# A transformer layer with 32 routed experts: gathers issued at other places, the long form of one expert in line, and a weight ring of 19 slots in place of 17

## The chip, the cores and the metric

The kernel runs on one core of one Trainium2 chip. The metric is device time in microseconds of one execution. The kernel before has a median of 1142.95 us over three runs (1142.18 to 1146.23).

## What is computed

One decoder layer over 256 tokens of width 1024 in float32: a mixer (three kinds of attention, a convolution, an output projection), a LayerNorm, and a mixture of 32 experts, of which each token takes four, closed by a second LayerNorm. The experts are what this case is about:

```python
def moe_ffn(x, router_w, router_b, w_gu, b_gu, w_down, b_down):
    t = x.reshape(B * L, D)
    logits = (t @ router_w + router_b).astype(jnp.float32)
    top_val, top_idx = lax.top_k(logits, TOP_K)            # TOP_K = 4
    wts = jax.nn.softmax(top_val, axis=-1)
    gates = jnp.sum(jax.nn.one_hot(top_idx, N_EXPERTS) * wts[..., None], axis=1)
    for e in range(N_EXPERTS):                             # 32
        gu = t @ w_gu[e] + b_gu[e]                         # 1024 x 2048
        gate = jnp.minimum(gu[:, ::2], SWIGLU_LIMIT)
        up = jnp.clip(gu[:, 1::2], -SWIGLU_LIMIT, SWIGLU_LIMIT)
        h = (up + 1.0) * gate * jax.nn.sigmoid(gate * SWIGLU_ALPHA)
        out = out + gates[:, e:e + 1] * (h @ w_down[e] + b_down[e])   # 1024 x 1024
```

The weights of an expert are 12 MB. The router is skewed: with these inputs the largest expert has 161 tokens, two have none, and those two are neither loaded nor computed.

## The kernel before

The mixer comes first; its instructions are scheduled by hand in one stream per engine. `order` (L868) then ranks the experts by their number of tokens on the chip. The experts run in an order of ranks that is fixed in `_ORDER` (L86) and cut into 14 batches; below, e0, e1, ... are places in that order. A batch is one, two or four experts that share one gather, and `HOME` is how many groups of 32 tokens (passes) of each the gather covers: four for an expert that is alone, two in a pair, one in a batch of four. The first batch is e0 alone (92 tokens here, three passes), the second is e1 to e4 (ranks 13, 17, 21 and 25, one pass each), the third is e5 alone: rank 1, 161 tokens, six passes, more than its home of four.

**The weights.** An expert's weights are 12 tiles of 1 MB ("loads" below), c0 to c7 for the first product and c8 to c11 for the second. They go through a ring of 17 slots in SBUF: `RING` = 16 (L41), and `wx` (L820), which is allocated after the mixer; one of the 16 holds the rows `res` of the first LayerNorm until the accumulator is built from it. e0's 12 loads are issued by the mixer's `prefetch`, which keeps `KEEP` = 6 slots free for the mixer itself. From e1 on SP issues every load in order (`load`, L1446; the DMA is L1450), each behind a wait for the slot's last reader (`released`, L977, on PE's counter `REL`).

**An expert.** `place(e)` (L1319) issues what belongs to the place and then `either` (L1010) branches by the expert's number of tokens to one of two forms of `passes` (L1334): the short one for at most `HOME` passes, which stands in line, or the long one, which stands behind the whole program (`put_behind`, L1025) and branches back. In a form PE does the first product for all passes (`up`, L1058), transposes h (`h_trans`, L1094), and does the second product (`down`, L1107); DVE and ACT do the activation between them (`act`, L1075) and evacuate the result to `ys` (`evacuate`, L1133). `bias` (L1049) opens a bank with a one-hot tile `sels[e % 4]`, which POOL writes.

**Gather and scatter.** Tokens are gathered by matmuls with a one-hot matrix: DVE writes P (`start_batch`, L1156), PE multiplies in two halves of 16 matmuls (`gather_next`, L1312, at L859) and DVE evacuates to `XG` (L865). DVE also writes P times the gates, PG (`start_gates`, L1169); PE transposes it (`gates_of`, L1208) and, at the next batch's first expert, scatters `ys` with it (`scatter_before`, L1219), which DVE adds to `acc` (L1226). For an expert with more tokens than its home there is a second set: Px, PGx (`gates_x`, L1274), the gather into `XGx` (`gather_x`, L1262) and `scatter_x` (L1285). `gates_x` is issued at the place of each expert with a home of four, and PE's short form of such an expert begins with a wait for it:

```python
            elif h == 4 and t_:
                take(X, PPX)
                take(X, PGRX)
            for ks in ((0, 1), (2, 3), (4,)):
```

The gather of the next batch is issued in the last expert of a batch, between `act` and `h_trans`; in e5's long form `gather_x` and `scatter_before` come first.

Of the kernel before, what the change touches and what calls it, by code (L numbers as in the profile page):

```python
# [34 lines left out]
L, D, E, SLOTS = 256, 1024, 32, 32  # L35
# [2 lines left out]
LAMBDA_INIT = 0.8 - 0.6 * math.exp(0.0)  # L38
NEG = -1e30
BIG = 3e38  # L40
RING = 16  # L41
SLOT = 2048
KEEP = 6
CT = 16
# [47 lines left out]
NPASS = [-(-min(L, 4 * L // max(1, _r)) // 32) for _r in SIGMA]  # L92
NR = RING + 1
TAIL = 3
B_DOWN = 9
WARM5 = 8


# [65 lines left out]
def body(ctx, tc, nc, A, out):  # L164
# [650 lines left out]
    def one(name, *shape, dt=F32):  # L815
        return mo.tile([128, *shape], dt, name=name)
# [23 lines left out]
    PGx = one("PGx", 2, 2, 4, SLOTS)  # L840
    hs = [one(f"h{i}", 256) for i in range(2)]
    gc = one("gc", 256)
    sels = [one(f"sel{i}", 128) for i in range(4)]

    ysx = [t.rearrange("p (n a) b -> p n (a b)", n=4) for t in XGx]
    pgTx = hT8[:, 4:8].rearrange("p s j t -> p (s j) t")
# [150 lines left out]
    def program(X, kind):  # L997
# [9 lines left out]
        def more(e, p):  # L1007
            return X.If(count(e) > p * SLOTS)

        def either(e, near, far, here):  # L1010

            name, here = f"{kind}{e}", here or nc.cur_bb
            X.br_cmp(count(e), HOME[e] * SLOTS, name + "_few", name + "_many", "IS_LE")
            nc.switch_bb(name + "_few", parent=here)
            near()
            X.br(name + "_end")

            def there_():
                nc.switch_bb(name + "_many", parent=here)
                far()  # L1020
                X.br(name + "_end")
            behind.append((name + "_many", there_))
            nc.switch_bb(name + "_end", parent=here)

        def put_behind():  # L1025
# [23 lines left out]
        def bias(e, p):  # L1049
            if t_:  # L1050
                b = gu_bank(e, p)
                if e:
                    X.wait_ge(SEL, e)
                take(X, FREE[b], 2)
                for i, w in enumerate(bgs):
                    X.matmul(pb_[b], R(sels[e % 4]), R(w), start=i == 0, stop=False, skip_group_check=True)  # L1056

        def up(e, p, ks):  # L1058
            if not t_:
# [201 lines left out]

        def gather_x(e, b=0):  # L1262

            if HOME[e] + 4 * b < NPASS[e] and not s_:
                with more(e, HOME[e] + 4 * b):
                    if v_ and (b or HOME[e] < 4):
                        one_hot_x(e, b).then_inc(PPX)
                    if t_:
                        take(X, PPX)
                    for k0 in (0, 4):  # L1270
                        gather(Px, XGx[b], k0)
                    gather_x(e, b + 1)
# [37 lines left out]
                    gates_T(PG, pgT, n0)  # L1310

        def gather_next(e, k0):  # L1312
            i = BATCH[e]
            if last_of(e) and i + 1 < len(BATCHES):
                if t_ and k0 == 0:
                    take(X, PP)
                gather(P, XGs[(i + 1) % 2], k0)

        def place(e, here=None):  # L1319
            i = BATCH[e]  # L1320
            if compute:
                count(e)
            if first_of(e):
                start_gates(i)
            if last_of(e) and i + 1 < len(BATCHES):
                start_batch(i + 1)
            if HOME[e] == 4:
                gates_x(e, 0)
            if i and first_of(e):
                there(6, 7)  # L1330
            if compute:
                either(e, lambda: passes(e, HOME[e]), lambda: passes(e, NPASS[e]), here)

        def passes(e, end):  # L1334

            h = HOME[e]
            many = end > h
            if many:
                gather_x(e)
                if h < 4:  # L1340
                    gates_x(e, 0)
                scatter_before(e, (6, 7, 6, 7))
                gates_of(e)
            elif h == 4 and t_:
                take(X, PPX)
                take(X, PGRX)
            for ks in ((0, 1), (2, 3), (4,)):
                def part(p):
                    if ks[0] == 0:
                        if p == h:  # L1350
                            there(6, 7)
                        bias(e, p)
                    up(e, p, ks)
                if t_:
                    nested(e, part, end)
                    up(e, 0, ks)

            if end > 1:
                with more(e, 1):
                    for p in range(end - 1, 1, -1):  # L1360
                        with more(e, p):
                            up(e, p, (5, 6, 7))
                            act(e, p)
                            if p + 1 < end:
                                with more(e, p + 1):
                                    h_trans(e, p + 1)
                    up(e, 1, (5, 6, 7))
                    act(e, 1)
                    if end > 2:
                        with more(e, 2):  # L1370
                            h_trans(e, 2)
            up(e, 0, (5, 6, 7))
            act(e, 0)
            if end > 1:
                with more(e, 1):
                    h_trans(e, 1)
            if not many:
                scatter_before(e)
                gates_of(e)
                gather_next(e, 0)  # L1380
                if h < 4:
                    gather_next(e, 4)
                if e == B_DOWN:
                    b_down()
            h_trans(e, 0)
            if not many and e + 1 < E:
                bias(e + 1, 0)
            for cs in ((8, 9), (10, 11)):
                def part(p):
                    down(e, p, cs)  # L1390
                if t_:
                    nested(e, part, end, h)
                    nested(e, part, h)
                    down(e, 0, cs)
                if cs[0] == 8 and not many and h == 4:
                    gather_next(e, 4)
            if many:
                with more(e, h):
                    nested(e, lambda p: evacuate(e, p), end, h)
                    if v_ or s_:  # L1400
                        X.drain().then_inc(YX)
            nested(e, lambda p: evacuate(e, p), h)
            evacuate(e, 0)
            if many:
                if e + 1 < E:
                    bias(e + 1, 0)
                scatter_x(e)
                for k0 in (0, 4):
                    gather_next(e, k0)
                if e == B_DOWN:  # L1410
                    b_down()

# [21 lines left out]
        if kind == "POOL":  # L1434
            for tb in range(2):
                X.tensor_tensor(acc[:, tb], z[:, tb], res[:, 0], op=OP.mult).then_inc(ACC)
            for tb in range(2):
                X.wait_ge(ACC, tb + 1)
                X.tensor_tensor(acc[:, tb], acc[:, tb], res[:, 1], op=OP.add).then_inc(ACC)
            for e in range(1, E):  # L1440
                if e >= 4:
                    X.wait_ge(REL, 11 * (e - 4) + 2)
                X.tensor_copy(R(sels[e % 4]).rearrange("p (q s) -> p q s", q=4),  # L1443
                              sel_q[:, :, e:e + 1].to_broadcast([128, 4, SLOTS])).then_inc(SEL)
        if kind == "SP":
            def load(e, x, cs=range(12)):  # L1446
# [89 lines left out]
```

## Time and profile before

| | |
|---|---|
| median of three runs | 1142.95 us |
| profiled execution: time, span | 1149.52 us, 1147.7 us |
| PE busy, granted clock | 942.2 us (82%), 0.885 |
| DVE, ACT, POOL busy | 368.7, 173.7, 110.3 us |
| HBM read | 401.08 MB, 350 GB/s over the span |

The profile is of one execution. Times are from the span's start. A row of the timeline gives start, duration, engine, line, operation, out<-in and count, and in brackets how long the engine had been idle before it and what released it; "PEq" is PE's sequencer (branches and semaphore operations) and "issue" is idle time in which nothing that the profile shows was waited for. GB/s is what all DMA queues moved.

### The profile page before, as it was taken

To read this page: it belongs to the slowest core of one execution; us is meant where nothing else is said; L and a number is where in the kernel's file an instruction comes from. 1 tells how busy PE (TensorE), PEld (TensorE's weight loads), DVE (VectorE), ACT (ScalarE), POOL (GpSimd) and SP (SyncE) were. 2 spreads that over 40 slices of the span, in tenths; PEclk is the share of its full clock that TensorE was granted. 3 is DMA by queue.
4 is the path that set the end of the run, shared out by engine and by line. 5 is a ranking of instruction groups with operands and counts; after the bars stand their busy time and mean duration, and the time that the engine had idled before them with its cause. 6 is when DMAs were issued, how large, how long until landed. Compare 5 with 4: busy or idle time off the path is not lost. (4 is left out here: it accounts for less than half of the span.)

```text
span 1147.7 us, 21218 instructions
## 1 busy us (share of the span) xinstructions
PE 942.2 (82%) x8356; PEld 492.0 (43%) x8356; DVE 368.7 (32%) x895; ACT 173.7 (15%) x371; POOL 110.3 (10%) x98
## 2 busy tenths in 40 slices
PE   9888895896669999977789997668998999866682
PEld 8777682452153363522234552113544445411232
DVE  4899564231130332311113321012333333201214
ACT  5526430210000110110001110000111111100000
POOL 2796503000000000000000000000000000000000
PEclk9898897998779999977699998878999999977766
DMA  9434364799998546999999999999999999999971
GB/s 371 157 142 184 111 266 172 313 376 426 427 423 336 207 150 281 423 427 426 427 425 426 423 424 427 426 427 425 425 426 424 426 424 425 425 426 427 426 333 42
DMA packets 56865, 403.91 MB, mean 352 GB/s; under 512 B 6304, under 2 KB 6432, under 8 KB 8224
## 3 DMA queue, kind: packets, MB, share of 16 engines
q1 hardware_dynamic: 56448, 400.98, 84.1%
q8 instruction: 85, 1.39, 0.5%
q10 hardware_dynamic: 288, 1.18, 0.3%
q14 instruction: 44, 0.36, 0.1%
HBM read 401.08 MB, written 1.05 MB: 350 GB/s over the span
## 5 line engine op out<-in xcount | busy, mean ns | idle before, releaser
L1068 PE MATMUL moe<-w,XG 128*32 128x512 f32 x2704 | 360.1, 661 | 77.5 <-DMA w<-in_we_dram 77.3
L1068 PEld LDWEIGHTS moe<-w,XG 128*32 128x32 f32 x2704 | 80.7, 114 | 321.0 <-DMA w<-in_we_dram 172.8
L1124 PE MATMUL moe<-w,hT 128*32 128x256 f32 x2720 | 169.3, 395 | 10.6 <-DMA w<-in_we_dram 5.1
L1083 DVE TENSOR_SCALAR gc<-moe 128x256 f32<-128x256 f32 x49 | 20.8, 425 | 447.0 <-DVEq L975 447.0
L1124 PEld LDWEIGHTS moe<-w,hT 128*32 128x32 f32 x2720 | 94.5, 114 | 77.8 <-issue 25.2
L1092 ACT ACTIVATE h<-gc 128x256 f32<-128x256 f32 x49 | 20.4, 416 | 501.0 <-ACTq L975 500.9
L1443 POOL CAST sel<-sel_q 128x128 fp32r<-128x128 f32 x31 | 9.3, 302 | 837.6 <-PE moe L1068 837.6
L1143 DVE COPY ys<-moe 32x256 f32<-32x256 f32 x94 | 39.5, 421 | 154.5 <-DVEq L975 153.4
L1056 PE MATMUL moe<-bg,sel 128*128 128x512 f32 x100 | 40.8, 493 | 28.1 <-PEq L975 28.0
L1143 ACT ACTIVATE ys<-moe 32x256 f32<-32x256 f32 x94 | 35.3, 375 | 178.8 <-ACTq L975 178.2
L859 PEld LDWEIGHTS moe<-P,z 128*128 128x128 f32 x416 | 53.8, 212 | 15.9 <-issue 15.9
L859 PE MATMUL moe<-P,z 128*128 128x128 f32 x416 | 56.8, 299 | 4.0 <-PEq L975 4.0
L1219 PE MATMUL moe<-ys,pgT 128*128 128x256 f32 x224 | 56.0, 397 | 2.6 <-PEq L975 2.3
L263 PE MATMUL pj<-s,h 128*128 128x256 f32 (+1 forms) x272 | 51.5, 291 | 2.1 <-ACT sv L317 2.1
L865 DVE TENSOR_SCALAR XG<-moe,pk 128x128 f32<-128x128 f32 x104 | 35.5, 404 | 49.2 <-DVEq L975 49.0
L1219 PEld LDWEIGHTS moe<-ys,pgT 128*128 128x128 f32 x224 | 42.0, 197 | 17.1 <-issue 12.0
L1226 DVE TENSOR_TENSOR acc<-acc,moe 128x512 f32<-128x512 f32 x60 | 39.2, 683 | 17.5 <-DVEq L975 17.5
L263 PEld LDWEIGHTS pj<-s,h 128*128 128x128 f32 (+1 forms) x272 | 43.5, 196 | 2.9 <-ACT sv L317 2.4
L263 PE MATMUL pj<-s,l 128*128 128x256 f32 (+1 forms) x136 | 39.4, 290 | 0.6 <-DVE l L280 0.6
L1101 PE MATMUL moe<-pk,h 128*128 128x128 f32 x98 | 21.0, 298 | 19.0 <-PEq L975 19.0
L1056 PEld LDWEIGHTS moe<-bg,sel 128*128 128x128 f32 x100 | 17.1, 215 | 42.1 <-issue 42.1
L280 POOL TENSOR_TENSOR l<-w,h 128x2048 fp32r<-128x2048 f32 x5 | 30.3, 6070 | 16.7 <-ACT h L275 16.7
(289 smaller groups left out, 906.8 us busy)
## 6 DMA issues: line engine op xcount, KB each, us to landing
w<-in_we_dram SPq DMA_DIRECT2D x318, 1024.0 KB, 25.8
wx<-in_we_dram SPq DMA_DIRECT2D x21, 1024.0 KB, 26.2
res<-in_we_dram SPq DMA_DIRECT2D x21, 1024.0 KB, 26.0
w<-in_wi_dram SPq DMA_DIRECT2D x11, 1024.0 KB, 12.6
w<-in_wo_dram SPq DMA_DIRECT2D x4, 1024.0 KB, 6.0
xt<-in_xt_dram SPq DMA_DIRECT2D x4, 256.0 KB, 5.0
w<-in_wi_dram SPq DMA_DIRECT2D x4, 256.0 KB, 5.4
t<-in_t_dram SPq DMA_DIRECT2D x1, 1024.0 KB, 16.2
```

The costliest lines, as they stand in the source:

```text
L263: T.matmul(o, R(l[x]), R(r[y]), start=first and i == 0, stop=last and i == 2)
L280: eng.tensor_tensor(R(W[c][1]), view(tiles[c], c), W[c][0], op=OP.subtract)
L859: i = X.matmul(p[:, a], z[:, tb, k * 128:k * 128 + 128], P[:, tb], start=tb == 0, stop=tb == 1)
L865: i = X.tensor_scalar(XG[:, k], p[:, a], par("g1")[:, k:k + 1], par("b1")[:, k:k + 1], op0=OP.mult, op1=OP.add)
L1056: X.matmul(pb_[b], R(sels[e % 4]), R(w), start=i == 0, stop=False, skip_group_check=True)
L1068: i = X.matmul(gu[32 * q:32 * q + 32], xg(e, p, k), w[:, q], start=False, stop=k == 7, skip_group_check=True)
L1083: X.tensor_scalar(gc, g, 7.0, None, op0=OP.min).then_inc(GC)
L1101: i = X.transpose(q[:, j], hs[p % 2][:, j * 128:j * 128 + 128], ident)
L1124: i = X.matmul(y[o:o + 32], hT8[:, p, j, 32 * q:32 * q + 32], w[:, n * 256:n * 256 + 256], start=(j == 0 and q == 0), stop=(j == 1 and q = ...
L1143: i = X.tensor_copy(dst[o:o + 32, c], y[o:o + 32]) if v_ else X.activation(dst[o:o + 32, c], y[o:o + 32], AF.Copy)
L1219: i = X.matmul(p[:, n * 256:n * 256 + 256], g[:, 2 * (2 * m + n) + tb], y[:, 2 * m + n], start=True, stop=True, skip_group_check=True)
L1226: X.tensor_tensor(o, o, p, op=OP.add).then_inc(FREE[b], 2)
```

## The change

- `RING` is 18: with `wx` and the slot of `res` that makes 19 slots in place of 17. The 16 KB per partition come from a smaller area for POOL's DMA descriptors (`dynamic_dma_scratch_size=512`) and from one `sels` tile fewer (three in place of four).
- In batches of four experts the next batch's one-hot matrix is written at the second expert, and the two halves of the gather are issued in the second and the third, not both in the fourth.
- For an expert with a home of four (except e0) `gates_x` and `gather_x` are issued in the expert before it. PE takes `PPX` there, and `PGRX` only after `h_trans`; e0 takes both after its `h_trans`.
- For rank 1 (e5) the long form stands in line and the short one behind the program.
- `b_down` moves from e9 to e17.

```diff
-RING = 16
+RING = 18
-B_DOWN = 9
+B_DOWN = 17
-    sels = [one(f"sel{i}", 128) for i in range(4)]
+    sels = [one(f"sel{i}", 128) for i in range(3)]
@@ either
-            nc.switch_bb(name + "_few", parent=here)
-            near()
-            X.br(name + "_end")
-
-            def there_():
-                nc.switch_bb(name + "_many", parent=here)
-                far()
-                X.br(name + "_end")
-            behind.append((name + "_many", there_))
+            line, other = ("_many", "_few") if SIGMA[e] == 1 else ("_few", "_many")
+
+            def form(which):
+                nc.switch_bb(name + which, parent=here)
+                (few if which == "_few" else many)()
+                X.br(name + "_end")
+            form(line)
+            behind.append((name + other, lambda: form(other)))
@@ gather_x
+            if t_ and (b == 0 and HOME[e] == 4):
+                take(X, PPX)
...
-                    if t_:
+                    if t_ and (b or HOME[e] < 4):
                         take(X, PPX)
@@ gather_next
-            i = BATCH[e]
-            if last_of(e) and i + 1 < len(BATCHES):
+            i, j = BATCH[e], e - BATCHES[BATCH[e]][0]
+            if i + 1 < len(BATCHES) and (j == 1 + k0 // 4 if HOME[e] == 1 else last_of(e)):
@@ place
+                if four(e + 1):
+                    count(e + 1)
-            if last_of(e) and i + 1 < len(BATCHES):
+            if i + 1 < len(BATCHES) and (e - BATCHES[i][0] == 1 if HOME[e] == 1 else last_of(e)):
                 start_batch(i + 1)
-            if HOME[e] == 4:
+            if e == 0:
                 gates_x(e, 0)
@@ passes
+            if not many and four(e + 1):
+                gates_x(e + 1, 0)
             if many:
-                gather_x(e)
+                if h < 4 or e == 0:
+                    gather_x(e)
...
-            elif h == 4 and t_:
-                take(X, PPX)
-                take(X, PGRX)
...
                 if h < 4:
                     gather_next(e, 4)
+                if four(e + 1):
+                    gather_x(e + 1)
...
             h_trans(e, 0)
+            if not many and h == 4 and t_:
+                take(X, PGRX)
+                if e == 0:
+                    take(X, PPX)
@@ kernel
-    nc = _bacc.Bacc("TRN2", target_bir_lowering=False, num_devices=1)
+    nc = _bacc.Bacc("TRN2", target_bir_lowering=False, num_devices=1, dynamic_dma_scratch_size=512)
```

In the rows below, names are: moe the PSUM banks, XG and XGx the gathered tokens, w, wx and res slots of the ring, pk a table of constants (the identity among them), hT the transposed h, sel the one-hot tile of the biases, bg the biases; what stands in brackets is the semaphores that the row waits on. Line numbers after the change are one or more lower or higher than before it.

PE at the start of e0, behind the bias of its first pass. Before:

```order
L1004 TENSOR_LOAD cnt
L1004 ISA x2
L1013 COMPARE_AND_BRANCH
L1008 COMPARE_AND_BRANCH [waits ppx,pgrx]
L1056 MATMUL moe<-bg_67,sel_1598 128x512 [waits free2]
```

Now:

```order
L1004 TENSOR_LOAD cnt
L1004 ISA x2
L1013 COMPARE_AND_BRANCH
L1008 COMPARE_AND_BRANCH
L1055 MATMUL moe<-bg_67,sel_1598 128x512 [waits free2]
```

The wait for Px and PGx is gone from this place.

PE in e4 between the last tile of the first product and the transposition of h. Before:

```order
L859 MATMUL moe<-P,z 128x128 [waits pp,free6]
L859 MATMUL moe<-P,z 128x128 x7
L859 MATMUL moe<-P,z 128x128 [waits free7]
L859 MATMUL moe<-P,z 128x128 x7
L1101 MATMUL moe<-pk_66,h_1595 128x128 [waits hh]
```

Now:

```order
L1008 COMPARE_AND_BRANCH [waits ppx]
L859 MATMUL moe<-Px,z 128x128 [waits free6]
L859 MATMUL moe<-Px,z 128x128 x7
L859 MATMUL moe<-Px,z 128x128 [waits free7]
L859 MATMUL moe<-Px,z 128x128 x7
L1266 UNCONDITIONAL_BRANCH
L1100 MATMUL moe<-pk_66,h_1595 128x128 [waits hh]
```

The gather of e5's first four passes stands no longer here (it went to e2 and e3), and that of its further passes stands here.

PE at the head of e5's long form. Before, behind the program:

```order
L1008 COMPARE_AND_BRANCH
L859 MATMUL moe<-Px,z 128x128 [waits ppx,free6]
L859 MATMUL moe<-Px,z 128x128 x7
L859 MATMUL moe<-Px,z 128x128 [waits free7]
L859 MATMUL moe<-Px,z 128x128 x7
L1265 UNCONDITIONAL_BRANCH
L1219 MATMUL moe<-ys,pgT 128x256 [waits free7,free6,free0]
L1219 MATMUL moe<-ys,pgT 128x256
```

Now, in line behind e4's last branch:

```order
L1019 UNCONDITIONAL_BRANCH
L1013 COMPARE_AND_BRANCH [waits free7,free6]
L1218 MATMUL moe<-ys,pgT 128x256 [waits free7,free6,free0]
L1218 MATMUL moe<-ys,pgT 128x256
L1218 MATMUL moe<-ys,pgT 128x256 [waits free7]
```

The form now begins with the scatter.

## Rows read from the trace of the kernel before

**Rows 1.** Busy time by stage: PE, PEld, DVE, ACT, POOL (count), PE clock, DMA share, GB/s

```profile
180.00:250.00 70.00, 57.41 (x556) 27.60 (x560) 23.13 (x47) 11.03 (x21) 7.65 (x8) 0.87 0.75 301
250.00:360.00 110.00, 77.42 (x630) 35.45 (x624) 19.32 (x52) 6.60 (x16) 0.89 (x3) 0.84 1.01 425
360.00:440.00 80.00, 71.83 (x796) 34.57 (x792) 21.08 (x52) 9.84 (x26) 0.59 (x2) 0.98 0.46 166
440.00:1113.00 673.00, 566.43 (x5235) 245.22 (x5224) 160.55 (x416) 64.52 (x162) 6.31 (x21) 0.88 1.01 424
1113.00:1147.70 34.70, 13.66 (x114) 10.91 (x113) 13.63 (x21) 2.11 (x5) 1.10 (x2) 0.74 0.14 53
```

**Rows 2.** DMA queue and issues: count, KB each, median us from issue to landing

```profile
q1 hardware_dynamic: 56448, 400.98, 84.1%
...
w<-in_we_dram SPq DMA_DIRECT2D x318, 1024.0 KB, 25.8
wx<-in_we_dram SPq DMA_DIRECT2D x21, 1024.0 KB, 26.2
res<-in_we_dram SPq DMA_DIRECT2D x21, 1024.0 KB, 26.0
...
res<-in_rows_dram SPq DMA_DIRECT2D x1, 1024.0 KB, 5.1
```

**Rows 3.** Waits of PE from 440 to 1113 us: us in total, times, longest

```profile
PE moe L1068 <- DMA w<-in_we_dram: 65.1, 66, 3.7
```

**Rows 4.** Timeline of the start of e0, 176 to 236 us

```profile
177.79 8.59 DVE L1177 TENSOR_TENSOR PG<-P,gp 128x128 f32<-128x128 f32 x4 [1.59 <-issue]
...
179.84 0.51 SPq L1450 DMA_DIRECT2D wx<-in_we_dram  x1
...
187.69 0.61 DVE L1281 TENSOR_SCALAR PGx<-Px,gp 128x256 f32<-128x256 f32 x2
188.73 1.19 PE L1056 MATMUL moe<-bg,sel 128*128 128x512 f32 x2 [9.22 <-PEq L975]
...
197.49 6.34 SPq L1450 DMA_DIRECT2D w<-in_we_dram  x4
```

**Rows 5.** Waits of PE from 250 to 323.5 us (e2 to e4)

```profile
PE moe L1068 <- DMA w<-in_we_dram: 12.2, 11, 1.4
```

**Rows 6.** Timeline from the end of e4 to the first matmuls of e5

```profile
313.04 5.82 PE L859 MATMUL moe<-P,z 128*128 128x128 f32 x32
...
319.75 3.66 PE L1124 MATMUL moe<-w,hT 128*32 128x256 f32 x64 [0.19 <-PEq L975]
...
323.60 0.87 DVE L1143 COPY ys<-moe 32x256 f32<-32x256 f32 x2 [3.21 <-DVEq L975]
...
325.90 0.47 DVE L1258 TENSOR_SCALAR Px<-pk,Rp 128x128 f32<-128x128 f32 x2
...
329.31 1.62 PE L859 MATMUL moe<-Px,z 128*128 128x128 f32 x6 [5.91 <-PEq L975]
334.33 4.66 PE L859 MATMUL moe<-Px,z 128*128 128x128 f32 x26 [3.40 <-issue]
...
340.77 1.97 PE L1219 MATMUL moe<-ys,pgT 128*128 128x256 f32 x8 [1.78 <-PEq L975]
...
346.34 0.71 PE L1056 MATMUL moe<-bg,sel 128*128 128x512 f32 x2
```

**Rows 7.** Timeline in e5's second product and from its end into e6

```profile
402.87 7.31 PE L1124 MATMUL moe<-w,hT 128*32 128x256 f32 x130 [2.06 <-issue]
...
430.76 1.37 DVE L865 TENSOR_SCALAR XG<-moe,pk 128x128 f32<-128x128 f32 x4 [0.41 <-DVEq L975]
...
433.31 1.19 PE L1056 MATMUL moe<-bg,sel 128*128 128x512 f32 x2 [2.71 <-PEq L975]
...
438.52 23.29 SPq L1450 DMA_DIRECT2D w<-in_we_dram  x11
```

**Rows 8.** Waits of ACT in the mixer, 0 to 200 us

```profile
ACT h L275 <- DMA w<-in_wi_dram: 2.7, 3, 1.8
```

More of the change, by code (lines that the diff above doesn't have):

```diff
@@ L1008, in more, with either @@
             return X.If(count(e) > p * SLOTS)
-        def either(e, near, far, here):
+        def either(e, few, many, here):
             name, here = f"{kind}{e}", here or nc.cur_bb
             X.br_cmp(count(e), HOME[e] * SLOTS, name + "_few", name + "_many", "IS_LE")
-            nc.switch_bb(name + "_few", parent=here)
-            near()
-            X.br(name + "_end")
-            def there_():
-                nc.switch_bb(name + "_many", parent=here)
-                far()
+            line, other = ("_many", "_few") if SIGMA[e] == 1 else ("_few", "_many")
+            def form(which):
+                nc.switch_bb(name + which, parent=here)
+                (few if which == "_few" else many)()
                 X.br(name + "_end")
-            behind.append((name + "_many", there_))
+            form(line)
+            behind.append((name + other, lambda: form(other)))
             nc.switch_bb(name + "_end", parent=here)
@@ L1055, in bias @@
                 for i, w in enumerate(bgs):
-                    X.matmul(pb_[b], R(sels[e % 4]), R(w), start=i == 0, stop=False, skip_group_check=True)
+                    X.matmul(pb_[b], R(sels[e % 3]), R(w), start=i == 0, stop=False, skip_group_check=True)
         def up(e, p, ks):
@@ L1317, in gather_next, with four @@
                 gather(P, XGs[(i + 1) % 2], k0)
+        def four(e):
+            return e < E and HOME[e] == 4
         def place(e, here=None):
@@ L1409, in passes @@
                     gather_next(e, k0)
+                if four(e + 1):
+                    gates_x(e + 1, 0)
+                    gather_x(e + 1)
                 if e == B_DOWN:
@@ L1440, in program @@
             for e in range(1, E):
-                if e >= 4:
-                    X.wait_ge(REL, 11 * (e - 4) + 2)
-                X.tensor_copy(R(sels[e % 4]).rearrange("p (q s) -> p q s", q=4),
+                if e >= 3:
+                    X.wait_ge(REL, 11 * (e - 3) + 2)
+                X.tensor_copy(R(sels[e % 3]).rearrange("p (q s) -> p q s", q=4),
                               sel_q[:, :, e:e + 1].to_broadcast([128, 4, SLOTS])).then_inc(SEL)
```

## The prediction

> **What bounds the kernel now.** I read the stages first, because the shares of the whole span mix stages with different limits. From 440 to 1113 us the DMA moves 424 GB/s without a break, and so it does from 250 to 360; from 180 to 250 it moves 301 and from 360 to 440 only 166 [rows 1]. PE in the long stage waits for weights in small pieces, 65.1 us in 66 waits [rows 3]. So the end of the program is set by the weights: the moment at which the DMA begins to run without a break, plus what is left to load, plus the last 34.7 us behind the last load [rows 1]. The loads are 318 + 21 + 21 = 360 of 1 MB [rows 2], 30 experts of 12. At 424 GB/s one takes 1.0486 / 0.424 = 2.47 us. As a test: at the end of e5 72 loads are used up and the ring of 17 is full, which leaves 271 and the rows of the last LayerNorm, 272 x 2.47 = 672 us; the stage has 673. Time can be won only where the DMA stands still. Against 425 GB/s that is 70 x (1 - 301/425) = 20.4 us around e0 and 80 x (1 - 166/425) = 48.8 us around e5. In both places the ring is full and PE, which should free slots, is late.
>
> Then the timelines of these two places. At e0, PE stands 9.22 us before its second bias at 188.73; DVE finishes PGx at 188.30. PE waits for Px and PGx, which the short form doesn't use before e0's end, and they are late because DVE's four PG take 8.59 us. SP has filled the free slots by 179.84 and gets the next at 197.49, from e0's first tiles [rows 4]. Behind e4, the second product ends at 319.75 + 3.66 = 323.41, but e5's first product starts behind the bias at 346.34: PE waits 5.91 us, runs six matmuls, stops 3.40 us in the middle of a run with nothing to wait for, gathers, and scatters from 340.77 on [rows 6]. At e5's end DVE frees the gather's bank at 430.76 + 1.37 = 432.13, PE goes on at 433.31, and SP has a free slot again at 438.52 [rows 7].
>
> **The change, part by part.**
>
> *e0 starts without the wait.* Only the bias's bank is left to wait for, so PE's chain from e0 on starts 9.2 us earlier [rows 4], and with it every slot that e0 frees. The waits now stand behind e0's transposition, over 20 us after the 188.3 at which DVE is done: nothing. -9.2 us.
>
> *Two more slots in this stage.* Before e0 frees any, SP has five slots beside e0's twelve (one of them `res`, later); now seven. Two loads more lie in the ring before the wait, 2 x 2.47 = -4.9 us. Together the DMA is 14.1 us ahead when it runs without a break; the 20.4 us it stands still now bound this from above, PE's 9.2 from below. I take 14.1: it follows from both parts, and leaves 6 us for starting up and e0's last releases.
>
> *Does the lead reach e5?* e3 and e4 wait for weights, 12.2 us in the up products [rows 5], and while they do, e4's end moves with the DMA. The lead over PE is 4.9 us. The gather that moves into e2 and e3 is 5.82 us [rows 6], partly inside their waits for the activation. 12.2 - 4.9 - 5.8 = 1.5 is still above zero, so e4 stays bound by its weights and ends 14.1 us earlier.
>
> *From e4 to e5.* e4's own chain keeps its length: the gather of Px takes the place of that of P, 32 matmuls for 32. Then nothing stands before the scatter but the evacuation, done at 323.60 + 0.87 = 324.47. From the scatter to the bias it is 346.34 - 340.77 = 5.57 us, so the bias comes at about 324.7 + 5.6 = 330.3 in the old count, 16.1 us earlier. After an idle stretch the matmuls are slower (1.62/6 = 270 ns against 4.66/26 = 179), for which I take off 0.6: -15.5 us. Its lower end is 6.2: should the 5.91 and 3.40 be needed in any form, only the rest goes. Weights don't limit it: the first two tiles land about 5 us behind e4's last, and e5 uses a tile in six passes. The gap of 3.40 I read as the fetch of code after the branch out of line, since no wait is there and the next rows run closely. The Trainium skill, Runtime: NRT & Kernel Launch, section Instruction fetch mechanics, says that code is fetched ahead in sequence only and that a taken branch out of the fetched pages waits for a transfer; the trace agrees with its 3.40 us. By that rule the entry in line is free and the sum would be -36.1; the form's own branches around passes that aren't run break the sequence too, though, and are a rival below.
>
> *e5's end.* The branch back goes. Of the 2.71 us in [rows 7] DVE's evacuation explains all up to 432.13; the 1.2 behind it become about 0.2. -1.0 us, between 0 and 2.7.
>
> *The full ring behind e5.* When the DMA starts again the ring is full, now with 19 tiles: two loads fewer are left for the long stage. -4.9 us, as sure as that stage is bound by loads. It comes twice because the ring runs full twice, with PE as the bound between.
>
> *The rest at nothing.* Gathers and `b_down` in later batches lie in the long stage under the 65.1 us of waits for weights [rows 3]; without that cover it would be a few us each. Three bias tiles let POOL work two experts ahead, which hides its casts. In the mixer two loads come earlier; ACT waits 2.7 us for weights there [rows 8], so 0 to -2.7. POOL's smaller area: nothing, all weights run on a hardware queue [rows 2].
>
> The sum is -14.1 - 15.5 - 1.0 - 4.9 = -35.5 us. The profiled execution took 1149.5 and would take 1114.0. It is 6.6 us above the median of the runs; from the median the forecast is 1142.95 - 35.5 = **1107.5 us**, a ratio of 0.969. Of the 69.2 us in which the DMA stands still, 35.5 go and 34 stay, so they don't cap it.
>
> **The range.** Both ends of each: the lead 9.2 to 20.4, the entry 6.2 to 16.1, the exit 0 to 2.7, the full ring 4.9, the mixer 0 to 2.7. All low is -20.3 (1122.6), all high -46.8 (1096.1). I give 1096 to 1123.
>
> **Rivals.**
>
> *The stops for code stay* (12 in 100). The form has eight passes of code and six are run, so it still branches; [rows 7] show a stop of 2.06 us of the same kind inside the form, behind such a branch. If the entry keeps its 9.3 us, the time is 1116.8. Against it: e4's second product, in line, starts 0.19 us behind PE's last work [rows 6]. The rule of the Trainium skill, Runtime: NRT & Kernel Launch, Instruction fetch mechanics, on taken branches holds for these inner branches as for the one that goes.
>
> *e2 to e4 become bound by PE* (6). The margin above is 1.5 us. If the gathers there cost their 5.8 in full behind e0's 9.2, e4 ends only 3.4 earlier: -24.8, 1118.2. For it speaks the small margin; against it that part of the gather fits into the waits for the activation.
>
> *The ring isn't the limit* (5): SP's order or its waits keep two slots empty. Then 9.8 us fall away, 1117.3. Against it: SP issues within microseconds of a release [rows 4, 7].
>
> *The smaller area throttles the loads*, and the kernel gets slower (2). Now a load lands 25.8 us after its issue [rows 2], so over ten are under way. If SP's loads needed room there, fewer could be. One alone takes 5.1 us [rows 2], so two at a time still give 2.55 each; below 2.07 under way the stream slows, and one at a time costs 348 x (5.1 - 2.47) = 915 us, 2058. Against it: the queue is a hardware one and POOL issues no load. The Trainium skill, DMA: Bandwidth & Descriptors, section SWDGE vs HWDGE vs iDMA, says that loads from SP never touch the rings in SBUF; no run here shows that yet.
>
> **How the numbers follow.** The forecast has 72 in 100, the four rivals 25, and 3 are left for a loss elsewhere that eats the gain, in the mixer or in a stage that PE comes to bound. 0.5% is 5.7 us, about what a measurement of this kernel can tell from no change. All but the last rival and the remainder are faster: 95; the remainder splits into 2 for no change, and 1 that goes with the 2 for slower.
>
> **What would show it.** PE's second bias at about 179.5; 301 GB/s in the stage around e0 up to 380 or more; e4's second product ending near 309 and e5's bias near 317 with no run of Px matmuls between them; no stop of several us in the head of e5; the DMA without a break from about 408, and the last load near 1078. Wrong it would be if e5's bias came later than 325, if PE no longer waited for weights in e4, if the DMA stood still again behind 440, or if its rate in the long stage fell below 424 GB/s.

## The result, and the profile after

The change takes 1109.47 us, the median of four runs (1106.92 to 1114.13), against 1142.57 before: a ratio of 0.9714, with an interval of 0.9666 to 0.9762. On another chip the same pair gave 1109.56 and 1146.72, a ratio of 0.9667 (0.9649 to 0.9685). That is 33 to 37 us faster. The forecast was 1107.5, 35.5 us faster, in a range of 1096 to 1123.

The profiled execution took 1106.92 us, its span is 1103.8. It is the fastest of its runs, and the profiled one of before (1149.52) lay above all of its own, so the two spans differ by more (43.9 us) than the medians. The stages first, with the columns of [rows 1]; the stage borders are moved to where the same work now lies.

```profile
180.00:250.00 70.00, 65.67 (x702) 32.39 (x698) 24.09 (x58) 12.57 (x25) 4.41 (x7) 0.99 0.97 399
250.00:300.00 50.00, 38.09 (x313) 15.19 (x308) 10.05 (x28) 3.10 (x8) 0.59 (x2) 0.80 1.01 427
300.00:400.00 100.00, 90.10 (x932) 41.73 (x926) 26.06 (x64) 11.76 (x30) 0.29 (x1) 0.98 0.79 325
400.00:420.00 20.00, 20.00 (x190) 9.11 (x186) 5.71 (x12) 2.47 (x6) 0.29 (x1) 1.00 0.89 358
420.00:1070.00 650.00, 540.04 (x5076) 232.60 (x5066) 154.96 (x404) 61.87 (x156) 6.53 (x22) 0.91 1.01 425
1070.00:1103.80 33.80, 11.84 (x112) 9.12 (x112) 13.61 (x21) 2.11 (x5) 2.07 (x2) 0.78 0.16 64
```

Around e0 the DMA now moves 399 GB/s where it moved 301, and the long stage keeps its rate, 425. Against 425 GB/s it stands still for 70 x (1 - 399/425) = 4.3 us around e0, 100 x (1 - 325/425) = 23.5 around e5 and 20 x (1 - 358/425) = 3.2 behind it: 31 us, where 69.2 were before.

The waits of PE for weights in the long stage (414 to 1072 us; total, times, longest) are longer than in [rows 3], 79.9 us for 65.1, so this stage is bound by the loads as before:

```profile
PE moe L1067 <- DMA w<-in_we_dram: 79.9, 75, 3.8
```

The start of e0 in the timeline, against [rows 4]:

```profile
174.48 8.66 DVE L1176 TENSOR_TENSOR PG<-P,gp 128x128 f32<-128x128 f32 x4 [1.57 <-issue]
174.93 2.64 SPq L1466 DMA_DIRECT2D w<-in_we_dram  x5
174.98 2.50 PE L1055 MATMUL moe<-bg,sel 128*128 128x512 f32 x4 [3.06 <-PEq L975]
177.41 3.62 PE L1067 MATMUL moe<-w,XG 128*32 128x512 f32 x16
```

DVE's four PG still take 8.66 us, but PE doesn't wait for them: both biases stand in one row and the first product follows at 177.41.

From the end of e4 to e5, against [rows 6]:

```profile
291.71 1.93 PE L1067 MATMUL moe<-wx,XG 128*32 128x512 f32 x8 [0.47 <-DMA wx<-in_we_dram]
293.57 3.84 PE L859 MATMUL moe<-Px,z 128*128 128x128 f32 x32
...
301.53 1.07 PE L1123 MATMUL moe<-w,hT 128*32 128x256 f32 x16 [0.44 <-DMA w<-in_we_dram]
303.78 1.96 PE L1218 MATMUL moe<-ys,pgT 128*128 128x256 f32 x8 [1.18 <-issue]
306.06 1.97 PE L1218 MATMUL moe<-ys,pgT 128*128 128x256 f32 x8 [0.31 <-PEq L975]
...
309.47 0.71 PE L1055 MATMUL moe<-bg,sel 128*128 128x512 f32 x2
```

The gather of Px lies in e4. Behind e4's end at 301.53 + 1.07 = 302.60 PE stops 1.18 us for the evacuation, scatters with one stop of 0.31 us, and opens e5 at 309.47: 6.87 us, where before they were 346.34 - 323.41 = 22.93.

The way from e5 into e6, against [rows 7], and the last first product of the program:

```profile
389.33 3.81 PE L859 MATMUL moe<-P,z 128*128 128x128 f32 x32 [0.19 <-PEq L975]
393.29 1.36 DVE L865 TENSOR_SCALAR XG<-moe,pk 128x128 f32<-128x128 f32 x4 [0.42 <-DVEq L975]
395.98 1.19 PE L1055 MATMUL moe<-bg,sel 128*128 128x512 f32 x2 [2.84 <-PEq L975]
401.49 0.89 SPq L1466 DMA_DIRECT2D w<-in_we_dram  x2
...
1066.12 1.06 PE L1067 MATMUL moe<-w,XG 128*32 128x512 f32 x8 [0.78 <-DMA w<-in_we_dram]
```

PE still stops 2.84 us in front of e6's bias (2.71 before).

Four rows of these timelines serve as marks below, the same four in every kernel: A, e0's first bias (here 174.98); B, the last first-product tile of e4 (291.71); F, the bias of e6 at e5's end (395.98); G, the last first product (1066.12). A to B is the lead, B to F is the entry, e5 and its exit, F to G the loads that a full ring leaves. Whole times of one kernel lie up to 12 us apart; such stretches of one profiled execution scatter less and show where a gain lies, but A to B of kernels with the old code still lies between 129.2 and 133.4 (first three rows of the table below).

### The profile page after: what moved, and what is told of

The parts are those of the page before. It is cut to its first block, busy times and chain, and to the rows that moved or that the text cites. A ratio compares the mean times of both kernels' runs of the same rounds, so it can differ in the third digit from the quotient of the medians.

```text
span 1103.8 us, 21225 instructions
## 1 busy us (share of the span) xinstructions
PE 922.1 (84%) x8356; PEld 477.4 (43%) x8356; DVE 368.5 (33%) x895; ACT 173.4 (16%) x371; POOL 111.3 (10%) x98
## 3 DMA queue, kind: packets, MB, share of 16 engines
q10 hardware_dynamic: 288, 1.18, 0.3%
## 5 line engine op out<-in xcount | busy, mean ns | idle before, releaser
L1067 PE MATMUL moe<-w,XG 128*32 128x512 f32 x2672 | 356.1, 658 | 89.2 <-DMA w<-in_we_dram 88.4
L1067 PEld LDWEIGHTS moe<-w,XG 128*32 128x32 f32 x2672 | 79.9, 114 | 330.2 <-DMA w<-in_we_dram 189.3
L1123 PE MATMUL moe<-w,hT 128*32 128x256 f32 x2880 | 171.8, 388 | 15.8 <-DMA w<-in_we_dram 9.9
L1123 PEld LDWEIGHTS moe<-w,hT 128*32 128x32 f32 x2880 | 95.6, 112 | 86.2 <-issue 22.9
L865 DVE TENSOR_SCALAR XG<-moe,pk 128x128 f32<-128x128 f32 x104 | 35.5, 403 | 46.5 <-DVEq L975 46.4
L1225 DVE TENSOR_TENSOR acc<-acc,moe 128x512 f32<-128x512 f32 x60 | 39.0, 682 | 14.2 <-DVEq L975 14.1
L1067 PE MATMUL moe<-res,XG 128*32 128x512 f32 x168 | 23.5, 620 | 5.6 <-DMA res<-in_we_dram 5.6
```

The source lines that it names most:

```text
L865: i = X.tensor_scalar(XG[:, k], p[:, a], par("g1")[:, k:k + 1], par("b1")[:, k:k + 1], op0=OP.mult, op1=OP.add)
L1067: i = X.matmul(gu[32 * q:32 * q + 32], xg(e, p, k), w[:, q], start=False, stop=k == 7, skip_group_check=True)
L1123: i = X.matmul(y[o:o + 32], hT8[:, p, j, 32 * q:32 * q + 32], w[:, n * 256:n * 256 + 256], start=(j == 0 and q == 0), stop=(j == 1 and q = ...
L1225: X.tensor_tensor(o, o, p, op=OP.add).then_inc(FREE[b], 2)
```

## The experiments

Two kernels are the one before with one part of the change (e1, e6), six are the change with one part undone, and v1 is a further step. Ratios are to the kernel before on the same chip, the interval in brackets.

| kernel | median us | ratio | A to B | B to F | F to G |
|---|---|---|---|---|---|
| before | 1142.57 | | 132.9 | 122.1 | 673.5 |
| before, second profile | 1146.72 | | 133.4 | 122.0 | 674.9 |
| e6 before with the small area | 1144.87 | 0.9998 [0.9974, 1.0022] | 129.2 | 121.6 | 673.8 |
| e1 before with 19 slots | 1134.31 | 0.9917 [0.9885, 0.9949] | 127.8 | 122.4 | 669.0 |
| e2 change with 17 slots | 1121.59 | 0.9805 [0.9773, 0.9837] | 121.5 | 104.2 | 673.3 |
| e8 change with 18 slots | 1114.09 | 0.9730 [0.9695, 0.9764] | 118.5 | 104.6 | 674.2 |
| e3 wait back at e0 | 1119.46 | 0.9789 [0.9756, 0.9822] | 124.3 | 104.4 | 668.8 |
| e4 long form behind | 1121.55 | 0.9805 [0.9770, 0.9840] | 115.5 | 115.7 | 669.3 |
| e5 Px gather at e5 | 1117.27 | 0.9770 [0.9735, 0.9804] | 116.9 | 113.3 | 669.0 |
| e7 batch gathers back | 1114.67 | 0.9725 [0.9689, 0.9761] | 115.7 | 106.0 | 668.8 |
| the change | 1109.47 | 0.9714 [0.9666, 0.9762] | 116.7 | 104.3 | 670.1 |
| the change, second chip | 1109.56 | 0.9667 [0.9649, 0.9685] | 116.4 | 105.8 | 668.5 |
| v1 scatter later | 1107.08 | 0.9659 [0.9641, 0.9678] | 117.7 | 101.0 | 671.4 |

### The ring alone, the moves alone, one slot

e1 is the kernel before with the ring (and the small area and three bias tiles that make room for it), e2 the change without the two slots, e8 with one of them.

```diff
# e1, in before
-RING = 16
+RING = 18
-    sels = [one(f"sel{i}", 128) for i in range(4)]
+    sels = [one(f"sel{i}", 128) for i in range(3)]
-    nc = _bacc.Bacc("TRN2", target_bir_lowering=False, num_devices=1)
+    nc = _bacc.Bacc("TRN2", target_bir_lowering=False, num_devices=1, dynamic_dma_scratch_size=512)
# e2, in the change
-RING = 18
+RING = 16
# e8, in the change
-RING = 18
+RING = 17
```

> The kernel before with 19 slots, three bias tiles and the small area for POOL's descriptors, and no gather or form moved. My theory (the ring runs full twice, and each time two slots more are two loads more): the DMA's lead over PE grows by 4.9 us around e0, so from e0's first bias to e4's last matmul of the first product it is 132.9 - 4.9 = 128.0 us; from e4's end to e5's bias it stays 22.9 us; 4.9 us more come in the long stage; in all -9.8 us, ratio 0.991. Rival A, the slots aren't the limit: 132.9 us and ratio 1.000. Rival B, the slots count once only: -4.9 us, 0.996. Rival C, the small area throttles loads: the long stage moves less than 424 GB/s.

> The changed kernel with 17 slots as before; the moves, the form in line and the small area stay. My theory: e0 starts 9.2 us earlier and takes the DMA along, so from e0's first bias to e4's last matmul of the first product 132.9 - 9.2 = 123.7 us; e4's end to e5's bias about 7 us as in the changed kernel; ratio 1 - 25.7/1143 = 0.9775. Rival A (slots aren't the limit): 117 us and the changed kernel's 0.971. Rival B (the earlier start is lost without slots, since the DMA then stands still as long): 133 us, 0.986.

> The changed kernel with 18 slots in place of 19. My theory: each slot counts one load of 2.47 us at e0 and one in the long stage: from e0's first bias to e4's last matmul of the first product 116.7 + 2.5 = 119.2 us, from e6's first bias to the last matmul of a first product 671 us (673 with 17, 669 with 19), the time 4.9 us over the changed kernel's, ratio 0.9755. Rival (a threshold: 18 already let the DMA run through at e0): 117 us and ratio 0.973 or less.

e1 gains 10.4 us of medians, ratio 0.9917, so two slots are worth something alone; that the ring isn't the limit is refuted. e2's ratio of 0.9805 against the change's 0.9714 and 0.9667 is a loss of 10 to 16 us. The table shows both places. In the lead e2 differs from the change by the slots alone: 121.5 us against 116.7 and 116.4, about 4.9 (115.5 to 117.7 in the five profiles with 19 slots and the change's code of PE up to B). e1's lead of 127.8 is less clear, 1.4 to 5.6 under the three profiles without its slots. From F to G the four profiles with 17 slots have 673.3 to 674.9 us, the eight with 19 have 668.5 to 671.4; the means, 673.9 and 669.4, are 4.5 us apart. The forecast had 4.9 twice. In the stage around e0 the two show what each part does alone (e1, then e2):

```profile
180.00:250.00 70.00, 59.55 (x596) 29.18 (x600) 20.99 (x46) 11.03 (x21) 5.30 (x6) 0.89 0.83 332
```

```profile
180.00:250.00 70.00, 66.19 (x671) 31.45 (x672) 26.08 (x54) 12.19 (x24) 8.12 (x8) 0.97 0.92 367
```

301 GB/s become 332 with the ring, 367 with the moves and 399 with both.

e8 lies between e2 and the change in time and in its lead, as one slot of two should; its F to G of 674.2 doesn't show the slot (671 expected). One profile and an interval that overlaps the change's don't settle it, and the rival's 0.973 is not excluded.

### The small area alone

```diff
-    nc = _bacc.Bacc("TRN2", target_bir_lowering=False, num_devices=1)
+    nc = _bacc.Bacc("TRN2", target_bir_lowering=False, num_devices=1, dynamic_dma_scratch_size=512)
```

> The kernel before with the small area for POOL's descriptors and nothing else. My theory: no load of SP or ACT uses it, ratio 1.000 within 0.4%, a load lands 25 to 27 us after its issue, the stage from 450 to 1050 us moves 424 to 426 GB/s. Rival (SP's loads need room there): fewer loads under way, a shorter time from issue to landing, a rate below 424 GB/s and a longer time.

The ratio is 0.9998. The long stage moves what it moved, and a load takes what it took (below, the stage from 450 us on and the line of the loads):

```profile
450.00:1050.00 600.00, 511.67 (x4846) 223.63 (x4841) 144.79 (x376) 59.22 (x149) 6.29 (x21) 0.88 1.01 425
```

```profile
w<-in_we_dram SPq DMA_DIRECT2D x318, 1024.0 KB, 25.8
```

The area only makes room. The rule of the Trainium skill, DMA: Bandwidth & Descriptors, section SWDGE vs HWDGE vs iDMA, that loads issued from SP don't use the rings in SBUF, is borne out by this ratio.

### e0's wait back

```diff
+            elif e == 0 and t_:
+                take(X, PPX)
+                take(X, PGRX)
             for ks in ((0, 1), (2, 3), (4,)):
...
-            if not many and h == 4 and t_:
+            if not many and h == 4 and t_ and e:
                 take(X, PGRX)
-                if e == 0:
-                    take(X, PPX)
```

> The changed kernel with PE's wait for Px and PGx put back at the head of e0. My theory: PE's second bias comes 9.2 us later, the slots of e0 come free 9.2 us later, and the DMA loses 9.2 of its lead: from e0's first bias to e4's last matmul of the first product 116.7 + 9.2 = 126 us, and the time is 9 us over the changed kernel's, ratio 0.979. Rival (the DMA's lead comes from the slots; PE's earlier start only makes PE wait more in e3 and e4): at most 119 us, ratio 0.971 to 0.974.

0.9789, as expected. The wait returns at its place, and the stage around e0 falls from 399 GB/s to 351:

```profile
187.07 1.19 PE L1055 MATMUL moe<-bg,sel 128*128 128x512 f32 x2 [9.14 <-PEq L975]
```

```profile
180.00:250.00 70.00, 59.11 (x616) 28.25 (x620) 22.83 (x51) 11.78 (x23) 6.09 (x7) 0.93 0.88 351
```

A to B is 124.3 us, 7.6 to 7.9 more than with the change (9.2 expected), and B to F and F to G are untouched: most of the wait of 9.14 us reaches the end of e4.

### The long form behind the program again, or the gather of Px at e5 again

e4 undoes the first half of what shortened the entry, e5 the second (its diff here is of PE and its place; `gates_x` goes back with the gather).

```diff
# e4
-            line, other = ("_many", "_few") if SIGMA[e] == 1 else ("_few", "_many")
+            line, other = "_few", "_many"
# e5
-            if e == 0:
+            if HOME[e] == 4:
                 gates_x(e, 0)
...
-                if h < 4 or e == 0:
-                    gather_x(e)
+                gather_x(e)
...
-                if four(e + 1):
-                    gather_x(e + 1)
```

> The changed kernel with e5's long form behind the program again; the gathers stay where the change has them. My theory (the stops of 2.9 and 3.4 us were the fetch of code after the branch): from the end of e4's second product to e5's first bias 6.9 + 6.3 = 13.2 us in place of 6.9, and the time about 6 us over the changed kernel's, ratio 0.977. Rival (the stops belonged to the gather of Px, to DVE's writes ahead of it and to the slow clock): still about 7 us, ratio 0.971.

> The changed kernel with the writes and the gather of Px back in e5's own place; the form stays in line, e0's wait stays late, 19 slots. My theory (the 22.9 us from e4's end to e5's bias before were code fetch and the gather, each a part of its own): without the jump the gather starts about 3.3 us behind e4's end, takes 4.8, its evacuation 1.8 and the scatter 5.6, so 15.4 us, against 6.9 in the changed kernel and 18.3 with the gather moved and the form behind; no stop of more than 3 us without a wait; ratio about 0.979. Rival (the stops belong to the gather of Px wherever its code stands): 22 to 23 us, ratio 0.985.

Both are slower than the change, 0.9805 and 0.9770 (e5's interval overlaps that of the change's first runs, not that on the second chip). e5's entry (e4's end to e5's bias) is 16.06 us, near the 15.4 expected. In e4 only the place of the code differs, and the entry takes 18.25 us for 6.87, where 13.2 were expected. The timeline of e4's kernel at the scatter:

```profile
308.86 0.76 PE L1218 MATMUL moe<-ys,pgT 128*128 128x256 f32 x1 [5.27 <-PEq L975]
314.27 6.13 PE L1218 MATMUL moe<-ys,pgT 128*128 128x256 f32 x15 [4.65 <-issue]
```

The 16 scatter matmuls of the change are cut behind the first, by a stop of 4.65 us in which nothing is waited for, and the wait ahead of them is 5.27 in place of 1.18. What the stops are, PE's sequencer shows first. Its branch into the form is L1013; the view has the sequencer under PEld, PE's weight loads, and gives count, duration in ns (lowest, median, highest) and start. The change, then e4's kernel:

```profile
L1013 PEldq COMPARE_BRANCH  x1: 65/65/65, 301.8 to 301.8; - x1
```

```profile
L1013 PEldq COMPARE_BRANCH  x1: 5877/5877/5877, 302.7 to 302.7; - x1
```

In e4's kernel the record holds the wait for the evacuation as well, but DVE is done with that at 304.66 and the branch ends at 302.7 + 5.9 = 308.6. Two DMA queues carry instructions; on the page of e4's kernel they are (packets, MB, share):

```profile
q8 instruction: 87, 1.43, 0.5%
...
q14 instruction: 44, 0.36, 0.1%
```

q8 is the one that goes with PE. PE has 72 branch records of over half a microsecond in the 13 profiles; each ends 2.3 to 3.0 us behind the start of a packet of q8, but anywhere from 0.02 to 31.5 us behind one of q14. q8 has 85 to 87 packets in the five profiles whose long form stands behind the program (both of before, e1, e4, e6), and 83 or 84 in the other eight. In each of the five, a packet starts late in either stop of the entry: in e4's kernel at 306.1 and 312.0, in before at 326.3 and 331.9. The second one of e4's kernel, in the window from 312.0 to 312.5:

```profile
q8 instruction: 1, 0.02, 12.7%
```

The branch ends 2.4 us behind the first of them (at 308.6, in before at 328.8), and the second stop 2.3 to 2.4 us behind the second (at 314.27, in before at 334.33). The change has one packet here, at 302.2 (e4's kernel has this one too, at 303.7), and its stop ends with the evacuation, at 303.7; e5's kernel has one at 310.6, while PE gathers, and no stop behind it. So the stops are the transfer of PE's code. That is what the Trainium skill, Runtime: NRT & Kernel Launch, section Instruction fetch mechanics, says of a taken branch out of what was fetched ahead; the packets agree, and the price is this case's.

Why does that price differ, 18.25 - 6.87 = 11.4 us in e4 and 22.93 - 16.06 = 6.9 between before and e5 (7.7 to 8.2 with the entries of e1, e6 and before's second profile)? In e4's kernel the parts are 5.27 - 1.18 = 4.1 of the first stop, 4.65 of the second, 0.76 + 6.13 - 1.96 - 1.97 = 3.0 of slower matmuls, less 0.3 between the halves. The clock granted to PE shows the last one: after the first stop it stands at 0.50, its lower level of 1.2 GHz, and the 15 matmuls run at 0.57 (windows of e4's kernel, columns as in [rows 1]):

```profile
309.00:314.20 5.20, 0.62 (x1) 0.12 (x1) 0.00 (x0) 0.00 (x0) 0.00 (x0) 0.50 1.01 416
314.20:320.50 6.30, 6.23 (x16) 4.76 (x17) 2.06 (x3) 0.00 (x0) 0.00 (x0) 0.57 1.01 423
```

In before PE has to wait for DVE's one-hot of Px at that place anyway, and this hides part of the first stop. e5's kernel shows it with the form in line:

```profile
306.96 5.44 PE L859 MATMUL moe<-Px,z 128*128 128x128 f32 x32 [3.28 <-PEq L975]
```

There the wait is 3.28 us and the gather runs in one piece. So of before's 6.9 us, 5.91 - 3.28 = 2.6 are the first stop, 3.40 the second, and 1.62 + 4.66 - 5.44 = 0.8 the slower matmuls.

### The batch gathers back in the fourth expert

```diff
-            if i + 1 < len(BATCHES) and (j == 1 + k0 // 4 if HOME[e] == 1 else last_of(e)):
+            if i + 1 < len(BATCHES) and last_of(e):
...
-            if i + 1 < len(BATCHES) and (e - BATCHES[i][0] == 1 if HOME[e] == 1 else last_of(e)):
+            if i + 1 < len(BATCHES) and last_of(e):
                 start_batch(i + 1)
```

> The changed kernel with the gathers of a batch's successor back in the last of four experts, both halves, beside the gather of Px that the change puts there. My theory: up to e4's last matmul of the first product nothing changes (116 to 117 us from e0's first bias, since e4 is bound by its weights), and from there to e4's end 32 more matmuls of 120 to 180 ns lie on PE's path, 10.9 + 4 to 5.5 us less half a microsecond of waiting for weights: 14.5 to 16 us; the time about 4 us over the changed kernel's, ratio 0.975. Rival (the gathers in e2 and e3 made PE the bound there): e4's last matmul comes earlier by 2 us or more and the time stays at 0.971.

The interval holds the expected 0.975 and the change's 0.9714 alike, so the runs don't tell. In the stretches, B to F grows by 0.2 to 1.7 us against the two profiles of the change, and A to B shrinks by 0.7 to 1.0: with the whole gather behind B in e4, B to e4's end grows from 10.89 to 13.07 us, not to the 14.5 to 16 expected, and the sum by 0.7 us at most and not by 4. What covers it there wasn't taken apart.

### A further step: e5's own scatter, later

B to F still holds e5's scatter at its end, behind which the DMA stands still. v1 issues it at the end of e6.

```diff
+            late = e and SIGMA[e - 1] == 1
+            if many and late:
+                scatter_x(e - 1)
...
-                scatter_x(e)
+                if SIGMA[e] != 1:
+                    scatter_x(e)
...
+            elif late:
+                scatter_x(e - 1)
```

> The changed kernel with the scatter of e5's passes beyond its home moved from e5's end to the end of e6 (at e6's head if e6 takes its long form). My theory (behind e4 PE's chain sets when the DMA starts again, and PE has slack once it runs): the 6.6 us of this scatter, 382.9 to 389.3 us in the changed kernel, leave the path up to e6's first slots, so from e5's first bias to e6's bias 86.5 - 6.5 = 80 us in place of 86.5, and the time falls by 6 us, ratio 0.966. Rival (e6 and e7 are as late as e5, and the DMA stands still there instead): 80 us too, but a pause of the DMA of several us between e6 and e7 and the changed kernel's 0.971.

> The changed kernel once more, to see what its marks scatter by, and beside the others on this chip. My theory: from e0's first bias to e4's last matmul of the first product 116 to 118 us, e4's end to e5's bias 6.9, e6's bias to the last matmul of a first product 669 to 670; ratio 0.970 to 0.973. Rival (one of the terms was an accident of that profile): one of these marks off by over 3 us.

On one chip v1 has 0.9659 [0.9641, 0.9678] and the change 0.9667 [0.9649, 0.9685]: no gain that can be measured. Counted from e5's first bias (309.47, in v1 310.24), the gather of the next batch begins at 383.70 - 310.24 = 73.5 us in place of 389.33 - 309.47 = 79.9, but the stop in front of e6's bias grows from 2.84 to 6.07 us and takes half of it back (83.3 us from e5's first bias to e6's, where 80 were expected):

```profile
383.70 0.49 PE L859 MATMUL moe<-P,z 128*128 128x128 f32 x3
387.59 1.37 DVE L865 TENSOR_SCALAR XG<-moe,pk 128x128 f32<-128x128 f32 x4 [0.42 <-DVEq L975]
...
393.50 1.19 PE L1055 MATMUL moe<-bg,sel 128*128 128x512 f32 x2 [6.07 <-PEq L975]
```

DVE is done at 388.96, 4.5 us ahead of the bias. PE's sequencer is still in the branch that closes the form:

```profile
L1019 PEldq COMPARE_BRANCH  x1: 7025/7025/7025, 385.3 to 385.3; - x1
```

It ends at 385.3 + 7.0 = 392.3, 2.3 us behind the start of a packet of q8 (390.0), so PE waits for code here; in the change the same branch takes 3.80 us. A packet had started at 386.8 already; why the branch ends only behind the second is open. The other half is lost behind e6, where the moved scatter lies on PE's path as well. v1 there, and the same first product in the change:

```profile
424.40 1.97 PE L1218 MATMUL moe<-XGx,hT 128*128 128x256 f32 x8 [1.25 <-PEq L975]
...
428.53 7.07 PE L1067 MATMUL moe<-w,XG 128*32 128x512 f32 x64
```

```profile
424.58 7.05 PE L1067 MATMUL moe<-w,XG 128*32 128x512 f32 x64
```

PE waits for no weights in these rows, so it had no slack: this product starts 428.53 - 310.24 = 118.3 us behind e5's first bias, against 424.58 - 309.47 = 115.1 in the change. Then the DMA dips, as the rival said, by 10 x (1 - 355/424) = 1.6 us' worth (v1, then the change):

```profile
430.00:440.00 10.00, 10.00 (x92) 5.52 (x80) 3.44 (x11) 0.69 (x2) 0.30 (x1) 1.00 0.94 355
```

```profile
430.00:440.00 10.00, 9.74 (x116) 6.73 (x108) 4.30 (x12) 0.80 (x2) 0.00 (x0) 1.00 1.01 424
```

F to G is 671.4 us, 1.2 to 2.9 more than with the change. No version was found that measurably beats the change.

A second profile of the kernel before was taken with these two (1146.51 us, span 1144.7); it is the second row of the table.

## Why the prediction was right, term by term

Taken from the stretches (means over the kernels that share a form; before and e6 on one side, the change's two profiles on the other): the lead 131.8 to 116.6, 15.2 us; B to F 121.9 to 105.0, 16.9 us; F to G 674.1 to 669.3, 4.8 us. Together 37 us, against a sum of 35.5 and measured 33 and 37. About one of them is given back outside the span: time and span lie 1.8 us apart in the runs of before and 2.6 to 3.2 in those of the change; the cause is open. None of the forecast's signs of being wrong appeared: e5's bias came at 309.47, e4 still waited for weights, and the DMA moved 425 GB/s from 420 us on.

- **The lead, -14.1, measured -15.2.** Both parts are there: the wait 7.6 to 7.9 (predicted 9.2, from e3), the two slots 4.9 (predicted 4.9, from e2), 12.5 to 12.8 together. The difference to 15.2 is within the scatter: before has 132.9 and 133.4, and e6, which differs from it by the small area alone, 129.2. That this is scatter and not the area is likely, since e6's ratio is 0.9998 and its profiled run (1141.18) lies 3.7 us under its median; three profiles don't settle it. That the forecast is met within a us or two is in part luck.
- **Does the lead reach e5?** Yes. e4 still waits for weights at B (0.47 us) and in its last product (0.44), and e2 to e4 didn't become bound by PE: that rival's -24.8 in all is refuted.
- **The entry, -15.5, measured 22.93 - 6.87 = -16.1.** It takes 22.9 to 24.2 us in the four profiles with the old entry and 6.8 to 8.3 in the seven with the new. The gain has two parts of known size, 9.2 us for the gather that moved (e5's 16.06 against 6.87) and 6.9 for the code that is fetched no longer. That the stops for code stay is refuted for the entry: in the change there is none up to the bias. Inside the form one is left, 1.28 us in the second product (2.06 in [rows 7]), in both 2.3 us behind the start of a packet of q8; the change's second profile has none over a us there. The deduction of 0.6 for slower matmuls after an idle stretch was not needed in the profile of the change; its second profile does show it (granted clock 0.70 from 306.38 to 312.03, the 16 matmuls 5.65 us in place of 3.9, the entry 8.3).
- **e5's exit, -1.0: this step failed.** The prediction let the branch back go and priced it at the 1.2 us behind DVE's evacuation. The stop is as long as it was, 2.84 us for 2.71 (2.36 in both second profiles), because the branch didn't go: `form` in the diff keeps `X.br(name + "_end")`, and PE still executes it. Its record in before, in the change and in e4's kernel:

```profile
L1021 PEldq COMPARE_BRANCH  x1: 3602/3602/3602, 428.5 to 428.5; - x1
```

```profile
L1019 PEldq COMPARE_BRANCH  x1: 3801/3801/3801, 391.0 to 391.0; - x1
```

```profile
L1019 PEldq COMPARE_BRANCH  x1: 3242/3242/3242, 403.9 to 403.9; - x1
```

  These end at 432.1, 394.8 and 407.1, v1's at 392.3, each 2.3 to 2.8 us behind the start of a packet of q8: the exit waits for code wherever the form stands. From there to e6's bias it is 1.2 to 1.3 us in all four (433.31, 395.98, 408.36 and 393.50), whether DVE ended 3.3 us before the branch (v1) or half a microsecond behind it (e4's kernel):

```profile
406.23 1.37 DVE L865 TENSOR_SCALAR XG<-moe,pk 128x128 f32<-128x128 f32 x4 [0.42 <-DVEq L975]
408.36 1.19 PE L1055 MATMUL moe<-bg,sel 128*128 128x512 f32 x2 [2.29 <-PEq L975]
```

  In this time PE's sequencer loads e6's count, compares and takes semaphores. So the 1.2 us are not the branch but what follows it; in before the branch ended within 0.1 us of DVE (432.13) and couldn't be seen beside it.
- **The full ring, -4.9, measured -4.5 to -4.8.** It counts a second time, as forecast.
- **Nothing for the rest.** The small area costs nothing (e6, 0.9998): the rival that throttles the loads is refuted. The gathers in batches of four are worth at most a us or two (e7). Whether the mixer gives anything is not settled: mark A lies between 174.8 and 178.6 us in all kernels but e8 (181.5), with either ring. `b_down` alone was not tried.

The stage around e5 still holds most of the 31 us in which the DMA stands. The change by tens of us from 360 on, last column GB/s:

```profile
360.00:370.00 10.00, 8.72 (x164) 5.10 (x155) 0.00 (x0) 0.19 (x1) 0.00 (x0) 1.00 0.66 274
370.00:380.00 10.00, 10.00 (x192) 6.86 (x185) 3.37 (x8) 3.00 (x8) 0.00 (x0) 1.00 0.55 213
380.00:390.00 10.00, 8.57 (x74) 5.90 (x67) 4.39 (x8) 2.58 (x6) 0.00 (x0) 1.00 0.58 210
390.00:400.00 10.00, 7.16 (x51) 4.23 (x53) 3.63 (x13) 0.00 (x0) 0.00 (x0) 0.83 0.03 6
```

PE is busy there at a granted clock of 1.00 for 30 us, with e5's six passes, and frees slots too slowly; only the last ten hold a gap, e5's scatter, gather and exit. v1 tried to shorten that and won nothing.

## What to carry to other kernels

Where a program is bound by a stream of loads through a ring, price an edit by when the stream runs without a break. Here most of a consumer's wait counted while the ring was full, and two slots counted about two loads at each of the two places where the ring runs full; gathers moved within batches counted for a us or two at most. Put the branch that the data always takes in line: the code of PE that was fetched behind such a branch cost 7 to 11 us here. PE's branch records and the packets of its own instruction queue tell such stops from other idle time, once it is clear which queue is PE's (q8 here, not q14). Before pricing a stop, read what the engine's sequencer does in it: at e5's exit 1.2 us were taken for a branch that they only followed, and the branch stayed. And work that is put off gains only if it lands where the engine waits (v1).

## What was not expected of the hardware

- A branch out of line cost two stops, not one: in the five profiles with it PE went on 5.3 to 6.2 us behind the end of its work ahead, ran one to six matmuls, and stopped again for 3.4 to 4.7 us, each time until 2.2 to 3.0 us behind the start of a packet of code.
- Such a wait for code needs no full DMA: the branch at e5's end took PE 3.80 us in the change, where the DMA was 0.03 busy (390 to 400 us), and 3.2 to 3.8 in every profile but v1.
- The stop is paid for again behind it: PE's granted clock was 0.50 in the 5.2 us behind e4's first stop, and the next 15 matmuls ran at 0.57 and took 409 ns each (6.13 / 15), against 246 in the change (3.93 / 16).
- Bringing e5's end forward by 6.4 us made the stop behind it 3.2 us longer (v1), with the branch there at 7.0 us in place of 3.8. Why it waits for a second packet is open.
